# The last norm in pieces of 256, 128 and 128 tokens, and its scaling four tiles at a time

## The chip, the cores and the metric

The kernel runs on one core of a Trainium2 chip. The metric is the device time of one execution in microseconds. Three runs of the kernel before took 1860.66, 1861.06 and 1865.96 us; their median is 1861.06.

## The reference

Two transformer blocks follow each other on 512 tokens of 1024 features, all in float32. The first is a mixer of several attention kinds and a gated feed-forward part with a convolution. The second has a short convolution, a feed-forward part (SwiGLU), latent attention, and a second SwiGLU, with a norm ahead of each. What matters here is the very end:

```python
h = h + swiglu_ffn(rms_norm_2(h, mla_ffn_norm_g[j]), w13, w2)   # (silu(g) * u) @ w2, w2: 2816 x 1024
return rms_norm_2(h, final_norm_g)                              # h * rsqrt(mean(h*h) + 1e-6) * g
```

The last norm needs the sum of squares over all 1024 features of a token before any of that token's outputs can be written.

## The kernel before

Activations lie transposed: features on the 128 partitions, tokens along the free dimension. The residual x is eight tiles of 128 features by 512 tokens. A weight matrix comes as column tiles; one column tile of the last product (w2) is 22 blocks of 128 x 128, loaded in three DMAs of 8, 7 and 7 blocks into `raw` (line 100). Each load is split into a high part `wh` (ScalarE, line 111) and the rest `wl` (VectorE, line 112), with two buffers of each. For each block `product` issues three matmuls into one bank of PSUM: high weights on high activations (line 125), high on low (line 126), low on high (line 127). Every matmul has its own weight load.

The last phase, `ffn2`, ends in `final`. Column tiles 0 to 6 are done on all 512 tokens: the product, the addition to x (line 332), the square (line 334), the running sum of squares `acc` on GpSimd (line 336), and x times the norm's vector, in place (line 337). The last column tile loads its weights once and goes over the tokens in two halves of 256. For each half come the product, the addition (line 344), the square (line 346), the scaling (line 347), and two matmuls with a matrix of ones (lines 351 and 352), which sum `acc` and the last square over the partitions. Then `rsqrt_wide` computes the factor r: Ln and Exp on ScalarE (lines 135 and 137), then four VectorE instructions (lines 139, 142, 143 and 145) of one Newton step.

`write` multiplies the eight tiles of x by r into tiles of the `raw` ring (line 365): of each four, three on VectorE and one on GpSimd. After each two it issues a DMA to the output on SyncE's queue (line 368), so eight of 256 KB in all. Half 0's `write` stands in the program after half 1's scaling and before half 1's matmuls with ones.

In this phase a scheduler orders each engine's instructions. It keeps program order among those that are ready, by its own model of their times; an instruction that waits for a buffer lets later ones of its engine pass. Once ordered, each engine works its list in order. Since the third weight load needs a buffer that holds the first eight blocks, TensorE's list goes on with half 1 on the first blocks before it ends half 0.

Of the kernel before, what the change touches and what calls it, by code (L numbers as in the profile page):

```python
# [9 lines left out]
F32 = mybir.dt.float32  # L10
# [4 lines left out]
ACTF = mybir.ActivationFunctionType  # L15
ALU = mybir.AluOpType
AX = mybir.AxisListType

S = 512
D = 1024  # L20
KD = D // 128
# [3 lines left out]
CHUNK = 8  # L25


class Builder:
# [294 lines left out]
    def final(self, w, xs, gi, out):  # L323


        nc = self.nc
        last = KD - 1
        g = [self.gains[:, gi * KD + k : gi * KD + k + 1] for k in range(KD)]
        acc = self.b("acc")
        for c in range(last):  # L330
            ps = self.dense(w, c, xs)
            nc.vector.tensor_tensor(out=self.x[c], in0=self.x[c], in1=ps, op=ALU.add)
            sq = acc if c == 0 else self.t(tag="sq")
            nc.scalar.activation(out=sq, in_=self.x[c], func=ACTF.Square)
            if c:
                nc.gpsimd.tensor_tensor(out=acc, in0=acc, in1=sq, op=ALU.add)
            nc.scalar.activation(out=self.x[c], in_=self.x[c], func=ACTF.Copy, scale=g[c])
        ws = self.weight(w, last, len(xs))
        n = S // 2
        for half in range(2):  # L340
            ts = slice(half * n, half * n + n)
            ps = self.product(ws, xs, ts)
            x = self.x[last][:, ts]
            nc.vector.tensor_tensor(out=x, in0=x, in1=ps, op=ALU.add)
            sq = self.t(tag="sq")[:, :n]
            nc.scalar.activation(out=sq, in_=x, func=ACTF.Square)
            nc.scalar.activation(out=x, in_=x, func=ACTF.Copy, scale=g[last])
            if half:
                self.write(out, 0, r)
            sp = self.pst()[:, :n]  # L350
            nc.tensor.matmul(out=sp, lhsT=self.ones, rhs=acc[:, ts], start=True, stop=False)
            nc.tensor.matmul(out=sp, lhsT=self.ones, rhs=sq, start=False, stop=True)
            r = self.rsqrt_wide(sp, 1.0 / D, None, n)
        self.write(out, 1, r)

    def write(self, out, half, r):

        nc = self.nc
        n = S // 2
        ts = slice(half * n, half * n + n)  # L360
        for i in range(2):
            y = self.raw.tile([128, CHUNK * 128], F32, tag="raw", name="raw").rearrange("p (k t) -> p k t", t=n)
            for k in range(4):
                eng = nc.gpsimd if k == 1 else nc.vector
                eng.tensor_tensor(out=y[:, k], in0=self.x[4 * i + k][:, ts], in1=r, op=ALU.mult)
                if k % 2:
                    ks = slice(4 * i + k - 1, 4 * i + k + 1)
                    nc.sync.dma_start(out=out[ks, :, ts].rearrange("k p t -> p k t"), in_=y[:, k - 1 : k + 1])


NH = 8
# [1195 lines left out]
@with_exitstack  # L1567
def kernel(ctx, tc, aps, out):
    b = Mix(ctx, tc, aps)
    with b.phase("mix", 2, s=4, sq=3, z=1):  # L1570
        b.start(0)
        b.mla_consts()
        b.mix_consts()
        b.mix()
    b.rope_pool = ctx.enter_context(tc.tile_pool(name="rope", bufs=1))
    with b.phase("ffn"):
        b.consts()
        b.conv_glu(2)
        b.conv_mixer(3)
        b.swiglu(5, aps["w13_a"], aps["w2_a"], b.rope_tables())  # L1580
    with b.phase("mla", 4, "pt"):
        b.mla(4, 6)
    with b.phase("ffn2"):
        b.swiglu(None, aps["w13_b"], aps["w2_b"], out=(7, out))


# [108 lines left out]
```

## Time and profile before

| what | us |
|---|---|
| median of three runs | 1861.06 |
| the profiled execution's own time | 1856.94 |
| its span, first to last instruction | 1855.1 |
| TensorE busy | 1817.0 |
| VectorE busy | 1055.4 |
| ScalarE busy | 737.9 |
| GpSimd busy | 193.8 |

The span is what the trace covers; the execution's own time is 1.84 us longer. Busy time is a share of the whole span and says little about its last part. Rows of the timeline give the start and the duration in microseconds, the engine, the line of the kernel, the operation, the tile written and those read, and the shapes; what stands in brackets is the idle time before it and what ended that. Matmuls are pipelined: the distance between two starts, not the duration, tells what one costs in a stream.

### The profile page before, as it was taken

The numbers are of one execution on the slowest core, as the hardware profiler recorded it, in microseconds if no ns is written. First come the engines' busy times: TensorE is split into PE (matmuls) and PEld (weight loads), VectorE is DVE, ScalarE is ACT, GpSimd is POOL, SyncE is SP. The second block draws the span as 40 slices with busy tenths as digits, with TensorE's granted clock in tenths as the row PEclk, the third lists the DMA queues.
The fourth block names the chain that finished last, engine by engine and source line by source line (L and its number), as shares of the span: only waits on it lengthen the run. The fifth ranks groups of instructions, "written<-read, shape, count | busy, mean of one in ns | idle before, by whom it ended". The sixth has DMA issues, their size and how long they took to land.

```text
span 1855.1 us, 22054 instructions
## 1 busy us (share of the span) xinstructions
PE 1817.0 (98%) x8609; PEld 1501.1 (81%) x8609; DVE 1055.4 (57%) x1627; ACT 737.9 (40%) x1138; POOL 193.8 (10%) x225
## 2 busy tenths in 40 slices
PE   8999999999999999999999999999999999999997
PEld 6787788778888888888888888888787888888886
DVE  7885976767777633555564444333876454444323
ACT  6544535454444422322342323323577333232322
POOL 1511402210000001111200000010011200000001
PEclk9999999999999999999999999999999999999999
DMA  5111110322223233232323232333212232323332
GB/s 168 57 42 40 48 38 30 120 95 96 99 95 102 86 96 103 91 102 92 102 96 103 91 102 92 94 97 105 64 57 75 79 103 91 102 91 99 94 94 77
DMA packets 53223, 162.61 MB, mean 88 GB/s; under 512 B 6528, under 2 KB 13184, under 8 KB 53120
## 3 DMA queue, kind: packets, MB, share of 16 engines
q1 hardware_dynamic: 52992, 161.21, 27.2%
q8 instruction: 67, 1.10, 0.2%
q14 instruction: 36, 0.29, 0.1%
q10 hardware_dynamic: 128, 0.01, 0.0%
HBM read 157.78 MB, written 2.10 MB: 86 GB/s over the span
## 4 chain that ended last, share of the span: by engine, by line
PE 86%; DVE 8%; ACT 4%; issue 1%; POOL 1%; DMA 0%; SPq 0%; DVEq 0%; POOLq 0%; ACTq 0%
PE mm L125 24%; PE mm L127 24%; PE mm L126 24%; PE mm L705 6%; PE gps L705 3%; PE lps L705 2%; PE fps L705 1%; DVE lbd L1317 1%; ACT wh L111 1%; DVE wl L112 1%; DVE lat L1368 1%; PE ps L577 0%; DVE ptl L112 0%; PE ps L165 0%; DVE nm L580 0%
## 5 line engine op out<-in xcount | busy, mean ns | idle before, releaser
L111 ACT ACTIVATE wh<-raw 128x1024 fp32r<-128x1024 f32 (+3 forms) x308 | 308.6, 1003 | 765.3 <-PE mm L126 459.4
L125 PE MATMUL mm<-xh,wh 128*128 128x512 f32 x1336 | 521.8, 391 | 0.4 <-ACT xh L173 0.4
L126 PE MATMUL mm<-xl,wh 128*128 128x512 f32 x1336 | 520.7, 390 | 0.5 <-DVE xl L174 0.5
L127 PE MATMUL mm<-xh,wl 128*128 128x512 f32 x1336 | 519.9, 389 | 0.0
L112 DVE TENSOR_TENSOR wl<-raw,wh 128x1024 fp32r<-128x1024 f32 (+3 forms) x300 | 362.1, 1207 | 226.0 <-ACT wh L111 222.9
L126 PEld LDWEIGHTS mm<-xl,wh 128*128 128x128 f32 x1336 | 250.8, 188 | 54.6 <-DVE xl L174 1.4
L125 PEld LDWEIGHTS mm<-xh,wh 128*128 128x128 f32 x1336 | 250.8, 188 | 53.7 <-issue 1.0
L127 PEld LDWEIGHTS mm<-xh,wl 128*128 128x128 f32 x1336 | 250.8, 188 | 52.1 <-issue 0.2
L125 PE MATMUL mm<-hidh,wh 128*128 128x512 f32 (+1 forms) x614 | 236.7, 386 | 0.0
L127 PE MATMUL mm<-hidh,wl 128*128 128x512 f32 (+1 forms) x614 | 235.3, 384 | 0.0
L126 PE MATMUL mm<-hidl,wh 128*128 128x512 f32 (+1 forms) x614 | 233.8, 381 | 0.0
L127 PEld LDWEIGHTS mm<-hidh,wl 128*128 128x128 f32 x614 | 115.4, 188 | 24.2
L705 PE MATMUL mm<-xh,wh 128*128 128x512 f32 x291 | 127.9, 439 | 6.8 <-ACT xh L173 6.0
L126 PEld LDWEIGHTS mm<-hidl,wh 128*128 128x128 f32 x614 | 115.4, 188 | 23.6
L125 PEld LDWEIGHTS mm<-hidh,wh 128*128 128x128 f32 x614 | 115.5, 188 | 21.9 <-ACT wh L111 0.2
L705 PE MATMUL mm<-xh,wl 128*128 128x512 f32 x291 | 116.1, 399 | 0.8 <-DVE wl L112 0.8
L705 PE MATMUL mm<-xl,wh 128*128 128x512 f32 x291 | 115.9, 398 | 0.4 <-DVE xl L112 0.4
L278 DVE TENSOR_TENSOR u<-mm,rb 128x512 f32<-128x512 f32 x44 | 30.4, 691 | 140.9 <-PE mm L127 140.9
L158 POOL TENSOR_TENSOR z<-z,sq 128x512 f32<-128x512 f32 x31 | 50.3, 1624 | 557.3 <-ACT sq L156 519.6
L274 DVE TENSOR_TENSOR u<-mm,rb 128x512 f32<-128x512 f32 x44 | 30.4, 691 | 90.9 <-PE mm L127 90.8
L111 ACT ACTIVATE hidh<-s 128x512 fp32r<-128x512 f32 x66 | 41.8, 633 | 88.3 <-DVE s L255 57.5
L705 PEld LDWEIGHTS mm<-xh,wh 128*128 128x128 f32 x291 | 56.5, 194 | 19.1 <-ACT xh L173 6.7
(434 smaller groups left out, 2087.3 us busy)
## 6 DMA issues: line engine op xcount, KB each, us to landing
raw<-in_w_a_dram SPq DMA_DIRECT2D x52, 512.0 KB, 3.3
raw<-in_w_b_dram SPq DMA_DIRECT2D x52, 512.0 KB, 3.3
raw<-in_w_up_dram SPq DMA_DIRECT2D x44, 512.0 KB, 3.3
raw<-in_w_in_dram SPq DMA_DIRECT2D x28, 512.0 KB, 3.3
raw<-in_conv_w_in_dram SPq DMA_DIRECT2D x24, 512.0 KB, 3.3
raw<-in_w_down_dram SPq DMA_DIRECT2D x16, 448.0 KB, 3.3
raw<-in_w_a_dram SPq DMA_DIRECT2D x16, 448.0 KB, 3.3
raw<-in_w_b_dram SPq DMA_DIRECT2D x16, 448.0 KB, 3.3
```

The costliest lines, as they stand in the source:

```text
L111: nc.scalar.activation(out=h, in_=src, func=ACTF.Copy)
L112: (eng or nc.vector).tensor_tensor(out=l, in0=src, in1=h.bitcast(F32), op=ALU.subtract)
L125: nc.tensor.matmul(out=ps, lhsT=h, rhs=xh, start=(k == 0), stop=False)
L126: nc.tensor.matmul(out=ps, lhsT=h, rhs=xl, start=False, stop=False)
L127: nc.tensor.matmul(out=ps, lhsT=l, rhs=xh, start=False, stop=(k == kt - 1))
L158: eng.tensor_tensor(out=acc, in0=acc, in1=sq, op=ALU.add)
L274: nc.vector.tensor_tensor(out=g, in0=ps, in1=r, op=ALU.mult)
L278: nc.vector.tensor_tensor(out=g, in0=ps, in1=r, op=ALU.mult)
L705: self.nc.tensor.matmul(out=out, lhsT=lhsT, rhs=rhs, start=start, stop=stop)
L1317: nc.vector.tensor_tensor(out=bd[rows, :, h].rearrange("p c (n j) -> p c n j", j=b), in0=c4(q)[rows], in1=c4(d)[rows], op=ALU.mult)
L1368: nc.vector.copy_predicated(out=at.rearrange("p c (n j) -> p c n j", j=2 * b)[:, :, :, b:], mask=self.lmask[:, lv - 1].rearrange("p (n j) ...
```

## The change

The last column tile goes over the tokens in three pieces, of 256, 128 and 128. The product of x with the norm's vector goes into a new tile of 128 x 4096 (`scaled_x`) instead of back into x. `write` multiplies four feature tiles at once by r, in place in that tile, all on VectorE; it issues one DMA for each four tiles, six in all, and the very last one on ScalarE's queue. A piece's `write` stands after the next piece's scaling, as before. The phase has one buffer with the tag z instead of two.

```diff
+        self.scaled_x = self.b("xg", shape=(128, KD * S)).rearrange("p (k t) -> p k t", t=S)
...
-            nc.scalar.activation(out=self.x[c], in_=self.x[c], func=ACTF.Copy, scale=g[c])
+            nc.scalar.activation(out=self.scaled_x[:, c], in_=self.x[c], func=ACTF.Copy, scale=g[c])
         ws = self.weight(w, last, len(xs))
-        n = S // 2
-        for half in range(2):
-            ts = slice(half * n, half * n + n)
+        r, old = None, None
+        for t0, n in ((0, 256), (256, 128), (384, 128)):
+            ts = slice(t0, t0 + n)
             ps = self.product(ws, xs, ts)
...
-            nc.scalar.activation(out=x, in_=x, func=ACTF.Copy, scale=g[last])
-            if half:
-                self.write(out, 0, r)
+            nc.scalar.activation(out=self.scaled_x[:, last, ts], in_=x, func=ACTF.Copy, scale=g[last])
+            if old:
+                self.write(out, old, r)
...
-            r = self.rsqrt_wide(sp, 1.0 / D, None, n)
-        self.write(out, 1, r)
+            r, old = self.rsqrt_wide(sp, 1.0 / D, None, n)[:, :n], ts
+        self.write(out, old, r)
...
         for i in range(2):
-            y = self.raw.tile([128, CHUNK * 128], F32, tag="raw", name="raw").rearrange("p (k t) -> p k t", t=n)
-            for k in range(4):
-                eng = nc.gpsimd if k == 1 else nc.vector
-                eng.tensor_tensor(out=y[:, k], in0=self.x[4 * i + k][:, ts], in1=r, op=ALU.mult)
-                if k % 2:
-                    ks = slice(4 * i + k - 1, 4 * i + k + 1)
-                    nc.sync.dma_start(out=out[ks, :, ts].rearrange("k p t -> p k t"), in_=y[:, k - 1 : k + 1])
+            ks = slice(4 * i, 4 * i + 4)
+            y = self.scaled_x[:, ks, ts]
+            nc.vector.tensor_tensor(out=y, in0=y, in1=r.unsqueeze(1).to_broadcast([128, 4, n]), op=ALU.mult)
+            eng = nc.scalar if i and ts.stop == S else nc.sync
+            eng.dma_start(out=out[ks, :, ts].rearrange("k p t -> p k t"), in_=y)
...
-    with b.phase("ffn2"):
+    with b.phase("ffn2", z=1):
```

## Rows read from the trace of the kernel before

**Rows 1.** The page: span and busy time of TensorE.

```profile
span 1855.1 us, 22054 instructions
PE 1817.0 (98%) x8609; PEld 1501.1 (81%) x8609; DVE 1055.4 (57%) x1627; ACT 737.9 (40%) x1138; POOL 193.8 (10%) x225
```

**Rows 2.** The chain of waits in the last part: start, us, what.

```profile
1839.91 0.66 PE ps L352 x2
...
1843.31 2.96 DVE raw L365 x6
...
1849.37 1.87 DVE raw L365 x4
```

**Rows 3.** The timeline of VectorE in the last part.

```profile
1838.88 0.42 DVE L344 TENSOR_TENSOR x<-x,mm 128x256 f32<-128x256 f32 x1 [2.62 <-PE mm L127]
...
1842.89 0.41 DVE L344 TENSOR_TENSOR x<-x,mm 128x256 f32<-128x256 f32 x1
1843.22 3.04 DVE L365 TENSOR_TENSOR raw<-x,s 128x256 f32<-128x256 f32 x6
1846.19 0.41 DVE L139 TENSOR_SCALAR s<-ps 128x256 f32<-128x256 f32 x1
...
1848.08 3.16 DVE L365 TENSOR_TENSOR raw<-x,s 128x256 f32<-128x256 f32 x6
```

**Rows 4.** Windows (engines' busy time, clock, DMA share, GB/s) and DMA issues (us to landing).

```profile
1850.00:1853.50 3.50, 0.00 (x0) 0.00 (x0) 1.24 (x4) 0.00 (x0) 0.00 (x0) 0.50 0.89 299
1853.50:1855.10 1.60, 0.00 (x0) 0.00 (x0) 0.00 (x0) 0.00 (x0) 0.00 (x0) 0.50 0.01 1
...
raw<-in_w_b_dram SPq DMA_DIRECT2D x52, 512.0 KB, 3.3
...
out_dram<-raw SPq DMA_DIRECT2D x8, 256.0 KB, 2.3
```

**Rows 5.** The timeline of TensorE in the last column tile.

```profile
1825.75 0.28 PE L125 MATMUL mm<-hidh,wh 128*128 128x256 f32 x1
...
1830.67 0.28 PE L127 MATMUL mm<-hidh,wl 128*128 128x256 f32 x1
1830.79 0.59 PE L351 MATMUL ps<-acc,ones 128*128 128x256 f32 x2
...
1831.34 0.28 PE L126 MATMUL mm<-hidl,wh 128*128 128x256 f32 x1
...
1842.43 0.28 PE L127 MATMUL mm<-hidh,wl 128*128 128x256 f32 x1
```

**Rows 6.** The timeline of ScalarE and TensorE around the third weight load.

```profile
1834.17 0.95 ACT L111 ACTIVATE wh<-raw 128x896 fp32r<-128x896 f32 x1 [6.41 <-PE mm L126]
...
1836.23 0.46 PE L127 MATMUL mm<-hidh,wl 128*128 128x256 f32 x2
```

**Rows 7.** The timeline of TensorE in the attention, products on 128 columns.

```profile
1352.86 0.23 PE L578 MATMUL ps<-negb,identb 128*128 128x128 bf16 x1
1352.90 0.42 PE L577 MATMUL ps<-kpeh,qr 128*128 128x384 f32 x1
...
1370.06 0.28 PE L577 MATMUL ps<-kpel,qr 128*128 128x128 f32 x1
...
1370.51 0.23 PE L578 MATMUL ps<-negb,identb 128*128 128x128 bf16 x1
```

**Rows 8.** VectorE: one operation of 1024 elements, then groups by form (mean ns).

```profile
1806.74 1.23 DVE L112 TENSOR_TENSOR wl<-raw,wh 128x1024 fp32r<-128x1024 f32 x1 [3.77 <-ACT wh L111]
...
L112 DVE TENSOR_TENSOR wl<-raw,wh 128x1024 fp32r<-128x1024 f32 x237 | 300.4, 1268 | 127.5 <-ACT wh L111 126.3
...
L1224 DVE TENSOR_TENSOR gx<-gx,gps 128x128 f32<-128x128 f32 x6 | 1.7, 288 | 1.9 <-PE gps L705 1.8
```

**Rows 9.** The timeline of ScalarE in half 1.

```profile
1843.40 0.42 ACT L346 ACTIVATE sq<-x 128x256 f32<-128x256 f32 x1 [1.88 <-DVE x L344]
...
1845.12 0.42 ACT L137 ACTIVATE u<-u 128x256 f32<-128x256 f32 x1
```

**Rows 10.** The z tile in the last phase: duration min/median/max, first and last start.

```profile
L153 ACT ACTIVATE z<-x x1: 619/619/619, 1443.0 to 1443.0; 128x512 f32<-128x512 f32 x1
```

More of the change, by code (lines that the diff above doesn't have):

```diff
@@ L352, in final, with write @@
             nc.tensor.matmul(out=sp, lhsT=self.ones, rhs=sq, start=False, stop=True)
-            r = self.rsqrt_wide(sp, 1.0 / D, None, n)
-        self.write(out, 1, r)
-    def write(self, out, half, r):
+            r, old = self.rsqrt_wide(sp, 1.0 / D, None, n)[:, :n], ts
+        self.write(out, old, r)
+    def write(self, out, ts, r):
         nc = self.nc
-        n = S // 2
-        ts = slice(half * n, half * n + n)
+        n = ts.stop - ts.start
         for i in range(2):
-            y = self.raw.tile([128, CHUNK * 128], F32, tag="raw", name="raw").rearrange("p (k t) -> p k t", t=n)
-            for k in range(4):
-                eng = nc.gpsimd if k == 1 else nc.vector
-                eng.tensor_tensor(out=y[:, k], in0=self.x[4 * i + k][:, ts], in1=r, op=ALU.mult)
-                if k % 2:
-                    ks = slice(4 * i + k - 1, 4 * i + k + 1)
-                    nc.sync.dma_start(out=out[ks, :, ts].rearrange("k p t -> p k t"), in_=y[:, k - 1 : k + 1])
+            ks = slice(4 * i, 4 * i + 4)
[3 more added lines that the diff above has]
+            eng.dma_start(out=out[ks, :, ts].rearrange("k p t -> p k t"), in_=y)
 NH = 8
```

## The prediction

> **What bounds the kernel now.** I read the page first: TensorE is busy for 1817.0 of 1855.1 us [rows 1]. The change, though, touches only the last column tile and what follows it, so the page's averages say little. The chain of waits tells where the end is set [rows 2]: it runs through TensorE's products until the ones-product of line 352 at 1839.91 and from there through VectorE, with the six multiplies of line 365 for half 0 (2.96 us) and the last four for half 1 (from 1849.37) at its end. VectorE's timeline [rows 3] shows the same stretch without a hole: from the addition of line 344 for half 1 at 1842.89 to the end of the last multiply at 1848.08 + 3.16 = 1851.24 it works for 8.35 us. The DMA windows [rows 4] show that data moved until about 1853.5 and that 1.6 us of closing work followed.
>
> One more thing has to be seen in TensorE's timeline. The tile needs 22 blocks of weights, in loads of 8, 7 and 7, and there are two buffers for them. The third load's split (line 111) can't start before every token piece has used the first eight blocks. So the order is: half 0 with blocks 0 to 14 until 1830.79 [rows 5], then half 1's blocks 0 to 7 (24 products), then the split at 1834.17 [rows 6], and half 0 goes on with block 15's third product at 1836.23 (two products stand in that row). Half 0 is complete, and its line 344 starts, at 1838.88 [rows 3]: 4.71 us after the split started.
>
> **The change, step by step.** The sum is made against the profiled execution, 1856.94 us with a span of 1855.1.
>
> *Pieces of 128 tokens on TensorE.* A product on 256 tokens has a pitch of 0.120 us: 41 pitches between 1825.75 and 1830.67 [rows 5]. The second half's 66 products become 132 on 128 tokens, each with its own weight load. The trace has such products in the attention: four in a row at 128 columns, from 1370.06 to 1370.51, so 0.1125 us each [rows 7]. Half the columns save nearly nothing; the pitch there belongs to the weight load. TensorE's extra work is 132 x 0.1125 - 66 x 0.120 = 6.93 us. The bounds of this pitch: 0.12 above; below, 0.04, at which a product follows a 128-column one of bf16 (1352.86 to 1352.90, rows 7). I take 0.1125, the row of the same kind and shape.
>
> The Trainium skill ("TensorE: Matmul & The Clock Gate", section "Back-to-back issue gap") gives about 81 ns per product at 128 columns in a stream of weight loads and products. The row shows 112 ns for it, so the page's figure is not what this kernel's products take. By the page's figure the whole sum below would end, as an estimate, at +2.8 us, 1863.8.
>
> *When piece 0 is complete.* This is the term that counts. Before the third split can start, TensorE must now do piece 1's blocks 0 to 14 (45 products, since they come earlier in the program and are ready), piece 1's ones-product of line 351, and piece 2's blocks 0 to 7 (24 products). Line 351 displaces (1831.34 - 0.12) - 1830.79 = 0.43 us on 256 tokens [rows 5]; on 128 I take 0.30, between half of it and all. So 45 x 0.1125 + 0.30 + 24 x 0.1125 = 8.06 us stand where 24 x 0.12 = 2.88 stood: the split moves by +5.18, to 1839.35, and piece 0's line 344 with it, to 1844.06. TensorE doesn't idle in this: piece 2's blocks 8 to 14 and block 15's first two products for two pieces are 25 x 0.1125 = 2.8 us, more than the 1836.23 - 1834.17 = 2.06 from split to use [rows 6]. Without that cover it would be a stall on top.
>
> *VectorE from there.* Piece 0's rsqrt is as before, 256 tokens wide, so line 344 of piece 1 stands at 1842.89 + 5.18 = 1848.07, behind it in VectorE's queue. Then, by rows: a multiply over four tiles has 1024 elements a lane for 256 tokens and 512 for 128. An undisturbed multiply-like operation of 1024 took 1.23 us (1.27 on average), of 128 it took 0.29 [rows 8]; 512 lies between them at 0.69. The bounds are that four tiles at once cost one pass (1.23), or four times a single tile of 256 (0.41 each, as the undisturbed ones in rows 3), 1.64. Successive independent instructions overlap by about 0.08 (0.41 long, next after 0.33: rows 3); the four of the rsqrt depend on each other and came 0.47 apart ((1848.08 - 1846.19) / 4), 0.05 more than they take; at 128 tokens 0.29 + 0.05 = 0.34. The list: line 344 of piece 1 0.21, write of piece 0 1.15 + 1.23 = 2.38, rsqrt of piece 1 1.36, line 344 of piece 2 0.21, write of piece 1 0.61 + 0.69 = 1.30, rsqrt of piece 2 1.36 and 0.11 in which it waits for its own Square, ones-products, Ln and Exp, write of piece 2 1.30. Sum 8.23 us, against 8.35: -0.12. The wait of 0.11: half 1's Square to the end of its Exp took 1845.12 + 0.42 - 1843.40 = 2.14 [rows 9]; with its four steps shorter by 0.1 each at 128 tokens it is 1.75, and beside it lie the write of piece 1 and line 139, 1.30 + 0.34. So the multiplies in fewer instructions, and without GpSimd (whose share now falls to VectorE), win as much as the third rsqrt and third addition cost, and little more.
>
> *TensorE's own end.* Last product at 1842.43 [rows 5], now some 7.3 us later, about 1849.8: piece 2's line 344 could start then, but VectorE comes to it only at 1848.07 + 0.21 + 2.38 + 1.36 = 1852.02. The 6.93 us are thus under VectorE's queue, which itself was pushed by 5.18.
>
> *Stores.* Eight stores of 256 KB become six: two of 512 KB, four of 256 KB with runs of 512 bytes, the last on ScalarE's queue, where nothing stands behind it. In the last stretch data moved at 299 GB/s over 3.5 us [rows 4], so half 1's megabyte kept the DMA engines full until 2.26 us after VectorE's end. Now only 512 KB come last; a store of 256 KB lands in 2.3 us [rows 4]. I take 2.15, -0.1. If runs of 512 bytes moved at half the rate, it would be +1.0.
>
> *At nothing:* scaling into the new tile instead of in place (the same operation and size), and one z buffer for two: this phase fills one z tile, once, at 1443.0 [rows 10].
>
> Sum: +5.18 - 0.12 - 0.10 = +4.96. Span 1855.1 to 1860.0; the profiled execution 1856.94 to 1861.9. The median of the runs shown, 1861.06, lies 4.1 above the profiled one; put on it, 1866.0 us, or 0.27% slower. About 0.3% (5.6 us) is what a measurement of this kernel can tell from no change, so I forecast a loss just under what can be told.
>
> **Rivals.**
>
> *A wait between the pieces' stores.* The multiplies now write in place in one tile, and a piece's four rows of tokens interleave with the other pieces' in address. If a multiply of piece 1 has to wait until piece 0's store has read the tile, it waits for a landing: 3.3 us for a load of 512 KB, 2.3 for a store of 256 [rows 4]. Piece 1's second multiply would start when piece 0's second store lands, about 1850.7 + 3.4 = 1854.1 for 1852.8, and piece 2's second when piece 1's does, at 1854.8 + 2.4 = 1857.2 for 1855.6: +1.6 on the forecast, 1867.6 us, 0.35% slower than before. It decides as soon as piece 0's second store lands over 2.1 us after its multiply. For it: the spans of addresses overlap. Against it: no byte is shared. Chance 0.15.
>
> *The pitch is the array's.* If 128 columns went in about 0.06, half of 0.12, because the weight load hides, the split would move by 45 x 0.06 + 0.2 + 24 x 0.06 - 2.88 = +1.46 and the whole by +1.2: 1862.3, no change that can be told; each 10 ns of pitch is worth 69 x 0.01 = 0.69 us, and at 0.041 nothing is lost. For it: the 0.04 of rows 7. Against: the four products beside it. Chance 0.10. The 81 ns of the Trainium skill (same page and section) would be a step towards this case.
>
> *A better order.* If TensorE takes piece 2's blocks 0 to 7 before piece 1's 8 to 14, the split comes 21 x 0.1125 = 2.36 earlier. Then TensorE's end binds: line 344 at about 1849.9, then 0.3 + 1.75 + 3 x 0.34 + 1.30 = 4.4 to VectorE's end, 1854.3 for 1851.24, and 0.1 off for the stores: +2.9, 1864.0. For it: nothing forbids it. Against: half 1 before took its blocks in order. Chance 0.15.
>
> **How the numbers follow.** My forecast has 0.55, with 1864.8 to 1867.2 as its own range; 0.05 is left for a gain I don't see. The range 1862.5 to 1869.0 takes in the order, the wait, 512-byte runs (+1.0) and multiplies at 1.64 (+0.8 in piece 0), and leaves out most of the array's pitch. Slower by over 0.3%: about 0.20 of the forecast (its upper third), 0.12 of the wait, 0.04 from the rest: 0.36. Faster by over 0.3% would need 5.6 us of the 12.6 after TensorE's products: 0.04. Within 0.3%: 0.60.
>
> **What would show it.** Right: products on 128 columns 0.11 apart; the third split near 1839.4; piece 0's line 344 near 1844; VectorE without a hole from 1848 to 1856.4; multiplies of 1.23 and 0.69; 2.1 us from its end to the last byte. Wrong: the split before 1838; a pitch under 0.09; VectorE waiting for a store's landing between the pieces, or for TensorE.

## The result, and the profile after

The kernel after took 1865.67 us (median of 22 runs, 1862.75 to 1875.48), the kernel before 1855.01 us (22 runs, 1852.90 to 1865.96). The ratio is 1.0052, 95% interval [1.0041, 1.0063]: the change costs 9.6 us by the ratio, 10.7 by the medians, about twice the 4.96 forecast. The predicted 1866.0 lies on the measured median only because two errors cancel. It was put on the median of the first three runs of before, 1861.06, which is 6.05 above that of all 22, and the change was forecast 4.7 to 5.7 us too cheap. That the median came out is luck.

The profiled execution of after took 1865.51 us. The page has, for [rows 1]:

```profile
span 1863.7 us, 22181 instructions
PE 1825.2 (98%) x8679; PEld 1509.5 (81%) x8679; DVE 1052.8 (56%) x1626; ACT 737.4 (40%) x1142; POOL 191.0 (10%) x221
```

The span grew by 8.6 us. I measure the tail of a kernel from the addition of column tile 6 (line 333 in after; the VectorE row of 128 x 512 elements just ahead of the last tile) to the end of the span. In after it starts at 1823.73 and is 39.97 long. In before it started at 1825.60 and was 29.50 long. So the tail grew by 10.47, and what lies ahead of it was 1.87 shorter in this execution. Everything below is inside the tail. VectorE in the last tile of after, for [rows 3] (start, duration, and in brackets the idle time before and what ended it):

```profile
1823.73 0.69 DVE L333 TENSOR_TENSOR x<-x,mm 128x512 f32<-128x512 f32 x1 [2.67 <-PE mm L127]
...
1842.06 0.42 DVE L345 TENSOR_TENSOR x<-x,mm 128x256 f32<-128x256 f32 x1 [2.62 <-PE mm L127]
...
1846.19 1.23 DVE L364 TENSOR_TENSOR xg<-xg,s 128x1024 f32<-128x1024 f32 x1
1847.34 0.28 DVE L345 TENSOR_TENSOR x<-x,mm 128x128 f32<-128x128 f32 x1
1847.54 1.22 DVE L364 TENSOR_TENSOR xg<-xg,s 128x1024 f32<-128x1024 f32 x1
1849.31 0.29 DVE L139 TENSOR_SCALAR s<-ps 128x128 f32<-128x128 f32 x1 [0.56 <-ACT u L135]
...
1850.68 1.29 DVE L364 TENSOR_TENSOR xg<-xg,s 128x512 f32<-128x512 f32 x2
1855.42 0.29 DVE L345 TENSOR_TENSOR x<-x,mm 128x128 f32<-128x128 f32 x1 [3.44 <-PE mm L127]
...
1858.71 1.29 DVE L364 TENSOR_TENSOR xg<-xg,s 128x512 f32<-128x512 f32 x2
```

Piece 0's addition is at 1842.06. Piece 1's, at 1847.34, stands behind the first multiply of piece 0. Piece 2's comes only at 1855.42, after VectorE had waited 3.44 us for TensorE. TensorE, for [rows 5]:

```profile
1837.57 0.28 PE L125 MATMUL mm<-hidh,wh 128*128 128x128 f32 x1
1838.37 0.39 PE L125 MATMUL mm<-hidh,wh 128*128 128x256 f32 x1 [0.53 <-ACT wh L111]
...
1839.49 0.38 PE L127 MATMUL mm<-hidh,wl 128*128 128x256 f32 x1 [0.22 <-DVE wl L112]
...
1843.05 0.70 PE L353 MATMUL ps<-sq,ones 128*128 128x256 f32 x2 [0.51 <-ACT sq L347]
...
1843.64 0.28 PE L127 MATMUL mm<-hidh,wl 128*128 128x128 f32 x1
...
1845.54 0.28 PE L126 MATMUL mm<-hidl,wh 128*128 128x128 f32 x1
1848.08 0.80 PE L353 MATMUL ps<-sq,ones 128*128 128x128 f32 x2 [2.26 <-ACT sq L347]
...
1848.78 0.41 PE L125 MATMUL mm<-hidh,wh 128*128 128x128 f32 x1
...
1854.96 0.41 PE L127 MATMUL mm<-hidh,wl 128*128 128x128 f32 x1
```

The last products ahead of 1845.54 are 0.112 apart (17 pitches from 1843.64). Then TensorE's list has piece 1's second ones-product (line 353), which needs the Square of piece 1 and so its addition. TensorE stands still for 2.26 us, with 31 of piece 2's 66 products queued behind. Such a wait of TensorE is called a stand below; three short ones came before it (0.53, 0.22 and 0.51). When those 31 go on they are 0.213 apart (29 pitches from 1848.78 to 1854.96). The windows show the clock (length; busy time of PE, PEld, DVE, ACT, POOL; granted clock; DMA share; GB/s), for [rows 4]:

```profile
1844.00:1846.00 2.00, 1.82 (x17) 1.67 (x15) 1.54 (x4) 0.68 (x2) 0.00 (x0) 1.00 0.03 8
1846.00:1847.00 1.00, 0.00 (x0) 0.00 (x0) 0.97 (x2) 0.00 (x0) 0.00 (x0) 1.00 0.00 0
1847.00:1848.00 1.00, 0.00 (x0) 0.00 (x0) 1.00 (x3) 0.29 (x2) 0.00 (x0) 0.52 0.00 0
1848.08:1855.20 7.12, 7.12 (x34) 7.12 (x34) 3.13 (x7) 0.91 (x3) 0.00 (x0) 0.50 0.70 221
```

During the stand the granted clock fell from 1.00 (2.4 GHz) to 0.50 (1.2 GHz), and it stayed there for the 7.12 us in which TensorE ended piece 2. The chain of waits now runs through exactly these (start, us, what), for [rows 2]:

```profile
1846.19 1.23 DVE xg L364
1847.42 0.21 DVE x L345
1847.71 0.32 ACT sq L347
1848.08 0.80 PE ps L353 x2
...
1855.42 0.30 DVE x L345
```

### The profile page after: what moved, and what is told of

The parts are those of the page before. It is cut to its first block, busy times and chain, and to the rows that moved or that the text cites. A ratio compares the mean times of both kernels' runs of the same rounds, so it can differ in the third digit from the quotient of the medians.

```text
span 1863.7 us, 22181 instructions
## 1 busy us (share of the span) xinstructions
PE 1825.2 (98%) x8679; PEld 1509.5 (81%) x8679; DVE 1052.8 (56%) x1626; ACT 737.4 (40%) x1142; POOL 191.0 (10%) x221
## 3 DMA queue, kind: packets, MB, share of 16 engines
q8 instruction: 68, 1.11, 0.3%
## 4 chain that ended last, share of the span: by engine, by line
PE 85%; DVE 8%; ACT 3%; issue 2%; DMA 1%; POOL 1%; SPq 0%; DVEq 0%; POOLq 0%; ACTq 0%
PE mm L125 24%; PE mm L127 24%; PE mm L126 24%; PE mm L703 6%; PE gps L703 3%; PE lps L703 2%; PE fps L703 1%; DVE lbd L1315 1%; ACT wh L111 1%; DVE wl L112 1%; DVE lat L1366 1%; PE ps L575 0%; DVE ptl L112 0%; PE ps L165 0%; DVE nm L578 0%
## 5 line engine op out<-in xcount | busy, mean ns | idle before, releaser
L125 PE MATMUL mm<-hidh,wh 128*128 128x512 f32 (+2 forms) x636 | 243.7, 383 | 0.5 <-ACT wh L111 0.5
L127 PE MATMUL mm<-hidh,wl 128*128 128x512 f32 (+2 forms) x636 | 242.8, 382 | 0.2 <-DVE wl L112 0.2
L126 PE MATMUL mm<-hidl,wh 128*128 128x512 f32 (+2 forms) x636 | 240.9, 379 | 0.0
L127 PEld LDWEIGHTS mm<-hidh,wl 128*128 128x128 f32 x636 | 121.1, 191 | 24.7 <-DVE wl L112 0.4
L126 PEld LDWEIGHTS mm<-hidl,wh 128*128 128x128 f32 x636 | 121.0, 190 | 23.6
L125 PEld LDWEIGHTS mm<-hidh,wh 128*128 128x128 f32 x636 | 121.2, 191 | 22.2 <-ACT wh L111 0.7
```

The source lines that it names most:

```text
L125: nc.tensor.matmul(out=ps, lhsT=h, rhs=xh, start=(k == 0), stop=False)
L126: nc.tensor.matmul(out=ps, lhsT=h, rhs=xl, start=False, stop=False)
L127: nc.tensor.matmul(out=ps, lhsT=l, rhs=xh, start=False, stop=(k == kt - 1))
```

## The experiments

All are single edits of after, unless said otherwise. For the tails, one profiled execution each is read; the median and the ratio to before are of the runs. The profiled execution isn't always a typical one: in "piece 2 early" and in "three pieces, own buffers" it is the fastest of all runs, in "addition first" the slowest.

**First the parts.** Is it the pieces, or the new write with its one tile? Halves of 256 with the new write:

```diff
-        for t0, n in ((0, 256), (256, 128), (384, 128)):
+        for t0, n in ((0, 256), (256, 256)):
```

> One part of the change alone: two halves of 256 tokens as before, with the new tile, the multiplies over four tiles at once and the fewer stores. Theory A (the loss is the pieces' alone, and the new write is a small gain): TensorE as in the kernel before; each write takes 2.4 us of VectorE instead of 3.0 to 3.2, so VectorE ends 1.3 us earlier; half 1's two stores of 512 KB start later after the multiplies than the four of 256 KB, which gives back 0.6. About 1854.3 us against 1855.0 before: within 0.3%. Theory B (the new write costs, through its strides, its in-place tile or its bigger stores): 2 us or more slower than before, 1857 us and up.

Measured: 1854.43 us (12 runs), ratio 1.0003 [0.9989, 1.0017]; tail 28.43. VectorE's writes of the two halves:

```profile
1841.35 2.35 DVE L364 TENSOR_TENSOR xg<-xg,s 128x1024 f32<-128x1024 f32 x2
...
1845.52 2.36 DVE L364 TENSOR_TENSOR xg<-xg,s 128x1024 f32<-128x1024 f32 x2
```

2.36 us stand where [rows 3] had 3.04 and 3.16. The write is 0.7 to 0.8 us shorter per half, and the time as a whole can't be told from before's.

The other part alone: before, with its old write, in three pieces.

```diff
-        n = S // 2
-        for half in range(2):
-            ts = slice(half * n, half * n + n)
+        r, old = None, None
+        for t0, n in ((0, 256), (256, 128), (384, 128)):
+            ts = slice(t0, t0 + n)
...
-            if half:
-                self.write(out, 0, r)
+            if old:
+                self.write(out, old, r)
```

> The other part of the change alone: three pieces of 256, 128 and 128, with the old write (one tile at a time into other tiles, a quarter of it on GpSimd). Theory A (the pieces carry the whole loss): as the changed kernel or 1 to 2 us more, since VectorE's writes are longer: 1865 to 1868 us. Theory B (the new write carries some of it): below 1863 us.

Measured: 1868.57 us (6 runs), ratio 1.0069 [1.0047, 1.009]; tail 42.58, the longest of all. TensorE's row of piece 1's second ones-product:

```profile
1851.05 0.79 PE L352 MATMUL ps<-sq,ones 128*128 128x128 f32 x2 [3.30 <-ACT sq L346]
```

So the pieces carry the whole loss. In the profile the stand is 3.30 us with the old write, not 2.26; that the new write hides a part of the loss isn't shown by the runs, since this interval overlaps that of after ([1.0041, 1.0063]). In this execution the clock also fell once ahead of any write (0.57 from 1840 to 1842).

**Then the stand.** Piece 0's multiplies put behind piece 1's addition on VectorE:

```diff
-            nc.vector.tensor_tensor(out=x, in0=x, in1=ps, op=ALU.add)
+            add = nc.vector.tensor_tensor(out=x, in0=x, in1=ps, op=ALU.add)
...
-                self.write(out, old, r)
+                with self.tc.issue_after(add.ins):
+                    self.write(out, old, r)
```

> The changed kernel with one order forced: the write of a piece queues on VectorE behind the next piece's addition to x. In the changed kernel TensorE stood still for 2.26 us before the ones-product of piece 1, since the addition of piece 1 waited on VectorE behind the first multiply of piece 0; after that still stand the granted clock was 0.50 and piece 2's products came 0.21 us apart instead of 0.11. Theory A (the still stand itself costs 2.26 us and brings the lower clock): the addition of piece 1 starts as soon as piece 0's rsqrt is done, the still stand falls to about 1 us, the clock stays at 1.00, piece 2's products come 0.1125 apart and end some 4.5 us earlier; VectorE has no hole any more and ends about as predicted for the change. Time about 1860.5 us, against 1865.7 of the changed kernel and 1855.0 of the kernel before. Theory B (products on 128 columns are too thin to hold the clock, whatever the order): the clock falls all the same, piece 2's products stay 0.21 apart, and only the shorter still stand is won: about 1864.4 us.

Measured: 1862.34 us (6 runs), ratio 1.0037 [1.0023, 1.0051]; tail 39.22. The time lies between theory A's figure (1860.5) and B's (1864.4). In the profile the stand shrank to 1.11 us, but it did not go: it ends with the Square, which needs the addition.

```profile
1848.27 0.49 PE L354 MATMUL ps<-sq,ones 128*128 128x128 f32 x2 [1.11 <-ACT sq L347]
```

The clock fell nevertheless, and in this execution twice:

```profile
1838.00:1840.00 2.00, 1.47 (x9) 1.33 (x8) 1.09 (x1) 0.67 (x1) 0.00 (x0) 0.73 0.00 0
1840.00:1842.00 2.00, 2.00 (x11) 2.00 (x11) 0.00 (x0) 0.00 (x0) 0.00 (x0) 0.50 0.00 0
1842.00:1844.00 2.00, 1.99 (x16) 1.85 (x15) 0.42 (x1) 0.00 (x0) 0.00 (x0) 0.91 0.00 0
...
1848.00:1849.00 1.00, 0.73 (x7) 0.73 (x7) 1.00 (x2) 0.71 (x3) 0.00 (x0) 1.00 0.00 0
1849.00:1850.00 1.00, 1.00 (x8) 1.00 (x8) 1.00 (x1) 0.48 (x2) 0.00 (x0) 0.59 0.02 7
1850.00:1852.00 2.00, 2.00 (x11) 2.00 (x11) 1.16 (x5) 0.00 (x0) 0.00 (x0) 0.50 1.02 342
```

The second fall follows the stand of 1.11. The first follows a stand of 0.53 at the third weight split, which after has too, at 1838.37, without a fall. This execution took 1865.12 us, the slowest of the six; the fastest took 1859.05, at a mean granted clock of 0.997 against its 0.993. So the falls seen here needn't be those of the median.

Next the stand was filled, with four products of ones on 256 columns that nobody reads:

```diff
+            if t0 == 256:
+                junk = self.pst("junk", 1)[:, :256]
+                for j in range(4):
+                    nc.tensor.matmul(out=junk, lhsT=self.ones, rhs=r, start=True, stop=True)
```

> The changed kernel with four more products of the matrix of ones with piece 0's r (256 columns, into a bank of their own that nobody reads) ahead of piece 1's ones-product on TensorE. They add work and leave the wait: piece 1's ones-product can't start earlier than in the changed kernel, since its addition still stands behind a multiply. Theory A (TensorE's idle time before it brought the lower clock): TensorE is busy for about 1.7 of the 2.26 us, the clock stays at 1.00, some 32 products of piece 2 come 0.1125 apart instead of 0.2135, and 3.2 us are won: about 1862.5 us. Theory B (the products on 128 columns lower the clock): the clock falls as before, 1865.7 us or a little more.

Measured: 1863.55 us (6 runs), ratio 1.0047 [1.0032, 1.0063]; tail 38.15. The filling needs r and so began only after a stand of 0.96 us, and the clock fell there already; it came back while the filling ran:

```profile
1845.64 3.41 PE L354 MATMUL junk<-s,ones 128*128 128x256 f32 x8 [0.96 <-DVE s L145]
```

```profile
1845.00:1846.00 1.00, 0.36 (x1) 0.36 (x2) 0.93 (x3) 0.00 (x0) 0.00 (x0) 0.56 0.00 0
1846.00:1848.00 2.00, 2.00 (x6) 1.55 (x6) 2.00 (x3) 0.60 (x2) 0.00 (x0) 0.50 0.06 20
1848.00:1849.00 1.00, 1.00 (x6) 0.86 (x5) 0.18 (x1) 0.00 (x0) 0.00 (x0) 0.73 1.03 343
1849.00:1851.00 2.00, 2.00 (x21) 2.00 (x19) 1.12 (x4) 0.68 (x2) 0.00 (x0) 1.00 0.99 333
```

A window of 2 us has 21 of TensorE's products at 1.00, against 11 at 0.50 in the run above. The test is inconclusive: the time is nearer to theory A's figure (1862.5) than to B's (1865.7) and the tail 1.8 us shorter than after's, but the clock fell all the same, and the interval overlaps that of after.

The clean way is to move the stand to where nothing is queued behind it: piece 2's products ahead of piece 1's two ones-products.

```diff
+        early = None
...
-            ps = self.product(ws, xs, ts)
+            ps = early if t0 == 384 else self.product(ws, xs, ts)
...
+            if t0 == 256:
+                early = self.product(ws, xs, slice(384, S))
```

> Piece 2's products stand before piece 1's two ones-products on TensorE; else as the changed kernel, products of 128 columns. This takes away the stand of 2.26 us and leaves the short ones (0.53, 0.22, 0.51). Theory A (the long stand lowers the clock): granted clock 1.00 to the last product; the last 50 products of the tile 0.1125 apart end near 1843.1 + 50 x 0.1125 = 1848.7, the addition of piece 2 is at about 1848.9 instead of 1855.42, both later factors are ready by 1851.6, the last multiply ends near 1853.7 and the span at 1857.4; the tail from column tile 6's addition 33.7 instead of 39.97, the time about 1859.4. Theory B (products of 128 columns with any stand beside them, short ones too): the clock falls to 0.5 behind the stand near 1838 or 1843 and the time stays at 1863 or above. My forecast's own term, TensorE's end under VectorE's queue, would be borne out by A: what the forecast missed is then the stand and its clock alone.

Measured: 1862.04 us (12 runs, 1858.70 to 1872.93), ratio 1.004 [1.0023, 1.0057]; the profiled execution took 1858.70, with a tail of 34.90. TensorE's windows and, from VectorE, piece 2's addition:

```profile
1836.00:1838.00 2.00, 1.35 (x9) 1.21 (x10) 1.09 (x1) 0.37 (x1) 0.00 (x0) 1.00 0.00 0
...
1840.00:1842.00 2.00, 1.49 (x12) 1.30 (x12) 0.42 (x1) 0.97 (x3) 0.00 (x0) 1.00 0.00 0
...
1846.00:1847.00 1.00, 1.00 (x11) 1.00 (x10) 0.82 (x1) 0.38 (x2) 0.00 (x0) 1.00 0.48 166
```

```profile
1847.38 0.29 DVE L346 TENSOR_TENSOR x<-x,mm 128x128 f32<-128x128 f32 x1 [0.56 <-PE mm L127]
```

The short stands (0.53, 0.23, 0.51) are still there and the clock held 1.00 to the last product, as theory A said; the profiled time is 0.7 below its 1859.4. Piece 2's addition is 25.38 after that of column tile 6, where after has 31.69. The median of the runs lies 2.6 above A's figure and 1 below B's bound: other executions have a lower mean granted clock (1858.70 us at 0.997, 1866.73 at 0.993, 1872.93 at 0.989). And the profiled execution is the fastest of the 12. So the long stand is shown to be a cause; that short ones never cost anything is not.

**Stand or thin products?** Pieces 1 and 2 computed on the 256 columns of the second half, half of each unread:

```diff
-            ps = self.product(ws, xs, ts)
+            wide = slice(256, S) if t0 else ts
+            ps = self.product(ws, xs, wide)[:, t0 - wide.start : t0 - wide.start + n]
```

> The changed kernel with the products of pieces 1 and 2 computed on 256 columns, of which only the piece's 128 are read: twice the columns for the same products, weight loads and pieces. Theory B (the thin products lower the clock): the clock stays at 1.00 in the whole tile, still stands of a microsecond or less included; the pitch is 0.12; TensorE's products take 132 x 0.0075 = 1.0 us more than the 22.8 they would take on 128 columns at full clock, and yet end earlier than in the changed kernel. VectorE's order differs in that the addition of piece 2 stands ahead of piece 1's rsqrt. About 1860.5 us, against 1865.7 of the changed kernel. Theory A (still stands lower it): as the run with the write behind the addition or a microsecond longer, 1862.3 us and up, with a granted clock of 0.50 over some microseconds.

Measured: 1859.90 us (12 runs), ratio 1.0026 [1.0011, 1.0041]; tail 34.52. Twice the columns in the same number of products, and faster than after: piece 1's addition came at 1845.63, ahead of the multiplies, and its ones-product at 1846.37 without any wait; the clock was 1.00 until 1852.

```profile
1844.00:1846.00 2.00, 2.00 (x18) 1.97 (x18) 1.14 (x4) 0.90 (x2) 0.00 (x0) 1.00 0.00 0
1846.00:1848.00 2.00, 1.99 (x16) 1.78 (x16) 1.93 (x4) 1.28 (x4) 0.00 (x0) 1.00 0.00 0
```

This had taken away thin products and stand together. The next puts a stand back among the wide products: as above, with piece 1's addition behind both multiplies and piece 2's last 21 products behind piece 1's second ones-product.

```diff
+                if t0 == 256:
+                    y = self.write(out, old, r)
+                    with self.tc.issue_after(y.ins):
+                        nc.vector.tensor_tensor(out=x, in0=x, in1=ps, op=ALU.add)
...
+            if after is not None and k == 15:
+                with self.tc.issue_after(after.ins):
+                    nc.tensor.matmul(out=ps, lhsT=h, rhs=xh, start=False, stop=False)
```

> Pieces 1 and 2 are computed on all 256 columns of the second half (half of each unread), as in the run with wide products; and piece 1's addition is put behind both multiplies of piece 0, with the last 21 products of piece 2 behind piece 1's second ones-product. So TensorE stands still once, for about 4.1 us, in a stream of wide products: from the last product of piece 1, near 1845.7, to the Square after an addition at 1842.53 + 4.1 + 2.4 = 1849.1, then 0.7 more. Theory A (a stand alone lowers the clock, whatever the width): granted clock 0.5 to 0.6 in the slice behind the stand and the 21 products about 0.22 to 0.24 apart, 4.6 to 5.0 us in all. Theory B (it takes products of 128 columns, with or beside a stand): clock 1.00 behind it, the 21 products 0.12 apart, 2.5 us. Time: from 1859.9, the addition of piece 2 comes at about 1849.9 + 2.5 + 0.2 = 1852.6 for 1849.4, and behind the write of piece 1: 1863 by B, 1865.5 by A.

Measured: 1865.06 us (6 runs), ratio 1.0053 [1.0033, 1.0072]; tail 39.41. TensorE:

```profile
1849.78 0.80 PE L363 MATMUL ps<-sq,ones 128*128 128x128 f32 x2 [3.10 <-ACT sq L357]
...
1850.59 0.41 PE L130 MATMUL mm<-hidl,wh 128*128 128x256 f32 x1
...
1854.64 0.41 PE L131 MATMUL mm<-hidh,wl 128*128 128x256 f32 x1
```

```profile
1848.00:1849.00 1.00, 0.00 (x0) 0.00 (x0) 1.00 (x1) 0.00 (x0) 0.00 (x0) 0.92 0.00 1
1849.00:1850.00 1.00, 0.22 (x1) 0.22 (x2) 0.32 (x2) 0.58 (x2) 0.00 (x0) 0.50 0.99 328
```

The stand was 3.10, not 4.1; behind it the clock was 0.50, and the wide products came 0.213 apart (19 pitches from 1850.59 to 1854.64), not 0.12. That is theory A's case, in the clock and in the time (1865.5 expected by A, 1863 by B). A long stand lowers the clock with wide products as with thin ones. No run has a stand of 0.5 to 2 us among the products of a tile with wide ones alone, so whether thin ones make a shorter stand enough isn't tested.

**The third weight load.** Last, the term of the forecast that counted, that the third split waits for all pieces' first blocks. The third load of the last tile gets buffers of its own, in after, in after with halves, and in before:

```diff
+            if own and i == n - 1:
+                for k in range(0, m, 4):
+                    j = min(4, m - k)
+                    h, l = self.parts(raw[:, k * 128 : (k + j) * 128], "x", KD, j * 128)
+                    out += [(h[:, a : a + 128], l[:, a : a + 128]) for a in range(0, j * 128, 128)]
+                break
```

> The changed kernel with the third weight load split into buffers of its own, as in the run of the kernel before with such buffers. No piece has to wait for another's products, so TensorE works through 66 products of 256 columns and then 132 of 128 with no still stand of note between them. The first four runs left two theories of TensorE's lower clock: in the run with the write behind the addition the clock fell twice (near 1838.5 and near 1849.5), in the one with the filled still stand once (near 1845.5) and then came back while piece 2's products ran. Theory A (it falls only after a still stand): here it stays at 1.00 through all 132, they come 0.1125 apart, TensorE's products end about 24.5 us after the tile's start, VectorE 4.4 us later; with 3.7 us for the stores and the end that is 32.6 us from the tile's start to the end, against 29.7 before: about 1858 us. Theory B (a run of products on 128 columns lowers it by itself): it falls within the 132, the pitch goes to 0.2135 for some tens of them, and the time is 1860 us or more.

> Two halves of 256, the third weight load in buffers of its own, and the new write: what the runs so far favour, put together. From the profiles, the time from the last tile's start to the end was 29.5 us before, 28.4 with the new write alone and 28.1 with the buffers alone. Theory A (the two gains lie in different places, the buffers' ahead of TensorE's end and the write's behind it): 27.4 to 27.8, about 1854 us, within 0.3% of before but the lowest of all runs. Theory B (the last half's megabyte of stores bounds the end in both): 28.1, no gain over the buffers alone.

> The kernel before with one wait removed: the last column tile's third weight load is split into buffers of its own (those of the normed activations, which are free by then), so that it needs no block of weights released by every token piece. Theory A (piece 0 is held by the second half's products on the first blocks): half 0 is complete 66 products after its start, about 5.5 us earlier than the 13.5 us after it of the kernel before; its rsqrt and its write pass under half 1's products; after TensorE's last product only half 1's chain is left, and VectorE ends some 1.2 us earlier: about 1853.8 us against 1855.0. Theory B (VectorE's and the stores' work bounds the end whatever comes first): no change, 1855.0 us.

Measured: three pieces 1858.53 us (10 runs), ratio 1.0021 [1.0002, 1.004], tail 32.80; halves with the new write 1852.66 us (12 runs), ratio 0.9988 [0.9974, 1.0002], tail 27.69; before with its old write 1854.99 us (12 runs), ratio 1.0001 [0.9985, 1.0016], tail 28.05. VectorE of the first:

```profile
1822.20 0.69 DVE L339 TENSOR_TENSOR x<-x,mm 128x512 f32<-128x512 f32 x1 [1.60 <-PE mm L133]
...
1830.11 0.42 DVE L351 TENSOR_TENSOR x<-x,mm 128x256 f32<-128x256 f32 x1 [6.06 <-PE mm L133]
...
1847.07 0.29 DVE L351 TENSOR_TENSOR x<-x,mm 128x128 f32<-128x128 f32 x1 [3.92 <-PE mm L133]
```

```profile
1842.00:1846.00 4.00, 4.00 (x39) 4.00 (x37) 1.15 (x2) 0.00 (x0) 0.00 (x0) 1.00 0.47 131
```

Piece 0's addition comes 7.91 behind column tile 6's, where after has 18.33. Yet the tail of three pieces is 5.11 longer than that of halves with the same buffers and the same write (5.87 by the medians): now VectorE waits for TensorE's last product in both (3.92 us here), and the thin products themselves are paid for. This run also shows thin products without a long stand (0.31, 0.22 and, after the last product, 0.45) at a clock of 1.00: in this execution thin products alone didn't lower it. In before the buffers alone win nothing that the runs show (theory B's figure was 1855.0), though the profiled tail is 1.45 shorter. The version with halves, new write and own buffers has the lowest median of all, but its interval reaches 1.

## Why the prediction was right or wrong

The runs side by side (tail, longest stand in the tile ahead of products, clock at the last products, median):

| kernel | tail | stand | clock | us |
|---|---|---|---|---|
| before | 29.50 | none | 1.00 | 1855.01 |
| after | 39.97 | 2.26 | 0.50 | 1865.67 |
| three pieces, old write | 42.58 | 3.30 | 0.50 | 1868.57 |
| addition first | 39.22 | 1.11 | 0.50 | 1862.34 |
| filled | 38.15 | 0.96 | 0.50, then 1.00 | 1863.55 |
| piece 2 early | 34.90 | 0.53 | 1.00 | 1862.04 |
| wide | 34.52 | none | 1.00 | 1859.90 |
| wide with a stand | 39.41 | 3.10 | 0.50 | 1865.06 |
| three pieces, own buffers | 32.80 | 0.31 | 1.00 | 1858.53 |
| halves, new write | 28.43 | none | 1.00 | 1854.43 |
| halves, new write, own buffers | 27.69 | none | 1.00 | 1852.66 |
| before, own buffers | 28.05 | none | 1.00 | 1854.99 |

*Pitch of 128 columns: right.* 0.112 in after, 0.1125 forecast. The rival "the pitch is the array's" falls. The Trainium skill ("TensorE: Matmul & The Clock Gate", section "LDWEIGHTS (loading the stationary operand)") puts the time of a weight load at its columns over 1.2, which makes 107 ns here as an estimate; the distance between two products agrees within 5 ns, better than with the 81 ns of the section that the prediction named. The row of a load itself lasts 190 ns in after, so the agreement is with the distance only.

*When piece 0 is complete: right.* Counted from column tile 6's addition, the third split (1837.37) moved by 13.64 - 8.57 = +5.07 for +5.18, and piece 0's addition by 18.33 - 13.28 = +5.05. The rival "a better order" didn't happen. The cover that the forecast put at 25 products didn't either: the split started at 1837.37, TensorE's last product ahead of its wait at 1837.57, and TensorE stood for 0.53 and 0.22 us.

*VectorE's prices: right.* The multiplies of piece 0 took 1.23 and 1.22, those of the others 1.29 a pair (1.30 forecast), the rsqrt on 128 tokens 1.37 to the multiply's start (1.36). No multiply waited for a store; that rival falls too.

*Stores: right.* From VectorE's last end (1860.00) to the span's end 3.70 us, 3.76 forecast.

*"TensorE doesn't idle" and "TensorE's own end ... under VectorE's queue": wrong, and in the profiles this is nearly the whole miss.* I looked for cover only at the third split, and took its order for granted there. I didn't ask what stands ahead of piece 2's last blocks in TensorE's list: piece 1's second ones-product, which needs an addition and a Square. And I put piece 1's addition ahead of piece 0's write; the scheduler's list had the first multiply ahead of it, 1.15 us. The forecast had VectorE at piece 2's addition 26.42 after column tile 6's; in after it is 31.69, so 5.27 late. From there to VectorE's end 4.58 passed for 4.28 forecast, and 0.06 came off at the stores: 4.96 + 5.27 + 0.30 - 0.06 = 10.47, the growth of the tail.

What the 5.27 consist of: TensorE's last product was forecast 24.2 after column tile 6's addition (1849.8) and came at 31.23, 7.03 late; 2.22 of it was slack in the forecast (1852.02 against 1849.8), and the addition starts 0.46 behind that product: 7.03 - 2.22 + 0.46 = 5.27. Of the 7.03 the long stand took 2.26, the lower clock 31 products times (0.213 - 0.112), 3.1, the short stands (0.53, 0.22, 0.51) that the forecast didn't have either 1.26; 0.4 is left for line 353 of pieces 0 and 1 in between. The trace can't split the stand's cost from its clock's by a run, since no run has such a stand and keeps 1.00; the two prices are worked out from rows. That both go with the stand is shown in a profile: with piece 2 early the tail is 34.90, 0.44 above the 29.50 + 4.96 of the forecast. That execution is the fastest of its runs; by the medians "piece 2 early" is 7.0 us slower than before, 2.1 more than the forecast, and no trace shows where these lie. "Wide", without any stand ahead of products, is 4.9 us slower by the medians, though its products and VectorE's order differ. So the sum described a kernel in which TensorE doesn't stand, and the scheduler's list wasn't that kernel.

The Trainium skill, same page, section "HAM oscillation — how this bites in real kernels", says that a kernel of thin products loses the higher clock through the pauses in which TensorE waits. The traces agree as to the pauses (2.26 us in after, 3.10 with wide products), though those of the Trainium skill's example are longer waits, for a DMA. They also show that a fall needs no thin products. I had read that page of the Trainium skill for its pitch and not for this.

*The chances: wrong side.* "Within 0.3%" had 0.60; the ratio's interval starts at 0.41% slower. I had taken 0.3% for the least that can be told; the interval reaches 0.11% to either side.

**Open:** why a stand of about 0.5 us was followed by a fall in the profiled executions of "addition first" and "three pieces, old write" (0.73 and 0.57 in the slices behind it), and not in those of after, "filled" and "piece 2 early", whose lists are the same up to there (but for a pair of ones-products that "piece 2 early" has later). It may be part of the spread between runs of one kernel.

## What to carry to other kernels

Before cutting a tile into thinner pieces, walk down TensorE's list and ask of each product that needs another engine's result what is queued behind it: its price is the stand plus the lower clock on all that follows, here 2.3 and 3.1 us. From 256 to 128 columns a product's pitch fell only from 0.120 to 0.112 us, so thinner pieces mostly add products. And a base should be taken from as many runs as the comparison will have: three runs put it 6 us too high, more than the forecast effect.

## What the runs showed of the hardware

At a granted clock of 1.00 products with a weight load each came 0.112 apart on 128 columns and 0.120 on 256 [rows 5]; at 0.50 both came 0.213 apart. After a fall the clock stayed at 0.50 through 7.12 us of products without a gap in after; in "filled" it was back at 1.00 from 1849, and in "addition first" the window from 1842 to 1844 has 0.91 after the first fall. What ran at the lower clock differs: in these two it was mostly products on 256 columns, and the clock came back, as it did behind the first fall of "three pieces, old write" (1.00 from 1844) and behind the wide products of "wide with a stand" (1.00 from 1856). Where products on 128 columns ran, in after, behind the second fall of "addition first" (1850 to 1855) and of "three pieces, old write" (1852 to 1858), it stayed at 0.50, busy as TensorE was. So the width seems to matter for the way back; no run was made to test that alone. The time of after follows the mean granted clock of the run: 1862.75 us at 0.995, 1872.18 at 0.990, 1875.48 at 0.987.
